# Retention's kept tiles on ScalarE's queue, and attention's gate by an exponential: a two-layer decoder in one launch

## The chip, the cores and the metric

The kernel runs on one core of one Trainium2 chip. The metric is the device time of one execution in microseconds (us), the median of three runs. Five engines work side by side, each in the order of its own instructions, and wait for each other by semaphores: TensorE (PE, with PEld for its weight loads), VectorE (DVE), ScalarE (ACT), GpSimd (POOL) and SyncE (SP). DMA transfers are issued by SP, POOL and, in the changed kernel, ACT, and run beside the engines.

## The reference

The trunk has two layers on 512 tokens of width 1024, all in 32-bit floats. Layer 0 mixes tokens by retention, layer 1 by forgetting attention. Each layer is: half a SwiGLU feed-forward, the mixer, half a SwiGLU feed-forward, a gated per-layer input. Cut to the two mixers:

```python
# retention, 4 heads, DK = 256, DV = 512
q, k, v, g = split(h @ w_in)
q, k = rotary(q), rotary(k) * DK ** -0.5
o = decayed causal (q k^T) v             # per head, decay gamma^(i - j)
y = silu(g) * rmsnorm(o, gn_w)           # norm over the head's 512 values
return y @ w_out

# forgetting attention, 16 heads of 64
q, k, v, fz = split(h @ w_in)
c = cumsum(log_sigmoid(fz + b_f))        # per head, over tokens
logits = q k^T * scale + c[i] - c[j]     # causal
return softmax(logits) @ v @ w_out
```

## The kernel before

Activations stand transposed, features on the 128 partitions and the 512 tokens along the row. Every product is made of three matmuls: each factor is split in a rounded half ("hi", a cast on ACT) and a rest ("lo", a subtraction on DVE), and hi·hi, hi·lo and lo·hi are summed in one of eight PSUM banks (`mm3`, L353 to L355). Feed-forward input products and most of retention's projections use one Strassen step (`product`, L557).

Weights are streamed by the class `Weights`: a plan lists all weight chunks in the order of use, SP loads a chunk raw, ACT casts its hi half (L88, or L134 and L135) and its lo half comes from DVE or POOL (L89), or from two ACT passes and an accumulating DMA on POOL (L136). There are three places for finished chunks; `take` gives the next chunk out and asks for those up to `look` (2) further on, so a chunk is cast when the chunk three before it has been used.

PE's order is that of the program text. The orders of the other engines are made by a planner at build time: among instructions that are ready in its own model of time it takes the one that stands earlier in the program. `tc.issue_after(x)` forces instructions of x's engine behind x. `with behind(last)` does so for a pair of instructions, one on ACT and one on DVE. On the chip each engine keeps the planned order, so an instruction whose input is late holds all that follow it on its engine.

Retention first makes q, k, v and gates of the heads 1 to 3 (and v of head 0) and keeps them in DRAM (`kept`, 28 pairs of tiles of 256 KB). Then, head by head: `scores` (four score blocks on PE, scaled and decayed by DVE at L911, split into `uhi` and `ulo` at L343 and L344), `attended` (48 matmuls of the split scores with v, the squares of the result on ACT at L937, their sum split), a part of the output projection of the head before (`out_blocks`), `head_scale` (mean of squares, root on ACT at L509, three Newton operations on DVE), more of the projection, `on_rows` (root to the rows: four PE transposes at L504 and an ACT copy at L957), and `outputs` (scale, gate, split). The next head's q, k and v come back from DRAM in `fetched`: a DMA on POOL (L853) puts a raw tile in what will be lo, ACT casts hi (L854), DVE subtracts (L855). `loaded(hd)` does it for a whole head; head 1's is called behind `attended` of head 0, later ones behind `attended` of the head before. The pool `ud` has 16 places: a head's q and k use 8 and its v 8 (4 of them elsewhere in heads 0 and 1).

Attention begins with the forget logits' product, `n.columns()` (root of the norm per token, in columns), the k product of the first pair of heads, `n.rows()` (columns to rows: PE transposes and an ACT copy), the q product. Then DVE and ACT work through log-sigmoid and cumulative sum on 16 rows, SP writes the sum to DRAM (`cdram`) and reads it back spread over all partitions (L1177). v is made in `v_block` (96 matmuls, split at L346 and L347), scores of pair 0 follow (L1169, L1172), softmax (DVE L1192 and L1196, ACT L1201 and L1203, POOL's causal mask L1178), then for each pair: k and q of the next pair, transposes of this pair's softmax (L1218), the product with v, scores of the next pair.

Of the kernel before, what the change touches and what calls it, by code (L numbers as in the profile page):

```python
# [18 lines left out]
S = 512  # L19
# [201 lines left out]
def trunk(ctx, tc, a):  # L221
# [18 lines left out]
    def unit(pool):  # L240
        return pool.tile([P, S], F32R, name="unit_" + {id(ua): "a", id(ub): "b", id(uc): "c", id(ud): "d"}[id(pool)])
# [265 lines left out]
    def rsqrt(out, v, t):  # L507

        root = nc.scalar.activation(t, v, AF.Sqrt)  # L509
        return root, newton(out, v, t)  # L510
# [8 lines left out]
    def mean_eps(out, total):  # L519
        nc.vector.tensor_scalar(out=out, in0=total, scalar1=1.0 / D, scalar2=EPS, op0=ALU.mult, op1=ALU.add)  # L520

    def proj(srcs, n, out=None, cols=slice(0, S), take=W.take):

        ws = [take(s) for s in srcs]
        os = out or [bank() for _ in ws]
        for k in range(KB):
            ks = slice(k * P, (k + 1) * P)
            for o, (wh, wl) in zip(os, ws):
                mm3(o, wh[:, ks], wl[:, ks], n.hi[k][:, cols], n.lo[k][:, cols], k == 0, k == KB - 1)
        return os  # L530
# [231 lines left out]
    def v_part(srcs, n):  # L762

        os = [bank() for _ in range(NT)]
        for c in range(4):
            wh, wl = W.take(srcs[c])
            for j in range(2):
                k = 2 * c + j
                js = slice(j * S, (j + 1) * S)
                for t in range(NT):  # L770
                    ts_ = slice(t * P, (t + 1) * P)
                    xh, xl = n.hi[k][:, ts_], n.lo[k][:, ts_]
                    nc.tensor.matmul(os[t], xh, wh[:, js], start=k == 0, stop=False)  # L773
                    nc.tensor.matmul(os[t], xh, wl[:, js], start=False, stop=False)  # L774
                    nc.tensor.matmul(os[t], xl, wh[:, js], start=False, stop=k == KB - 1)  # L775
        return os
# [16 lines left out]
    def retention(n, nxt, pools):  # L793
# [50 lines left out]
                nc.scalar.copy(t1, os[t])  # L844
                nc.gpsimd.dma_start(out=to[t // 2][:, t % 2, :], in_=t1)

        def fetched(src, low=ud, high=ud):

            out = []
            for s in range(2):  # L850
                hi, lo = unit(high), unit(low)
                raw = lo.bitcast(F32)
                nc.gpsimd.dma_start(out=raw, in_=src[:, s, :])  # L853
                nc.scalar.copy(hi, raw)  # L854
                nc.vector.tensor_tensor(out=lo, in0=raw, in1=hi.bitcast(F32), op=ALU.subtract)  # L855
                out.append((hi, lo))
            return out

        by7, got, dks = Strassen(n), {}, []

# [30 lines left out]
        sums.close()  # L891

        pool = stack.enter_context(tc.tile_pool(name="ret", bufs=1, reuse_waits="tile"))

        def loaded(hd):
            if hd == 0:
                return fetched(vd[0][0], ua) + fetched(vd[0][1], ua)
            q, kk = fetched(qd[hd]), fetched(kd[hd])
            return q, kk, fetched(vd[hd][0]) + (fetched(vd[hd][1], ub, ub) if hd == 1 else fetched(vd[hd][1]))

        def scores(hd, q, kk):
            dk, u = dks.pop(0), []
# [20 lines left out]
        @contextmanager  # L923
        def behind(last):
            with tc.issue_after(last[0].ins), tc.issue_after(last[1].ins):
                yield

        def attended(v, u):
            os = [bank() for _ in range(4)]
            for j in range(NT):  # L930
                for d, o in enumerate(os):
                    ds_ = slice(d * P, (d + 1) * P)
                    mm3(o[:, j * P : S], v[j][0][:, ds_], v[j][1][:, ds_], *u[j], j == 0, j == NT - 1)
            acc = None
            for d in range(4):
                sq = temp()
                nc.scalar.activation(sq, os[d], AF.Square)  # L937
                if acc is None:
                    acc = sq
                else:  # L940
                    nc.vector.tensor_tensor(out=acc, in0=acc, in1=sq, op=ALU.add)
            hi, lo = temp(F32R), temp(F32R)
            return os, (hi, lo), split(acc, hi, lo)

        def head_scale(parts):

            total = over_tokens(parts)
            v, t, rn = (pool.tile([P, NT], F32, name=x) for x in ("rv", "rt", "rn"))
            nc.vector.scalar_tensor_tensor(
                out=v, in0=total, scalar=1.0 / S, in1=epsc, op0=ALU.mult, op1=ALU.add  # L950
            )
            rsqrt(rn, v, t)
            return rn

        def on_rows(rn):
            rows = pool.tile([P, S], F32, name="rnrows")
# [44 lines left out]

        out_w, y = {}, [([], []) for _ in range(RH)]
        W.by_dma |= {id(x) for hd in (0, 1) for x in ret_o[hd]}
        v = loaded(0)
        u, _ = scores(0, got["q", 0], got["k", 0])
        sg = [gate(0)]
        os, acc, _ = attended(v, u)
        q, kk, v = loaded(1)
        sg.append(gate(1))
        rn = head_scale(acc)  # L1010
        (g,) = proj_forms(ret_g[0][2], n)
        rn, copied = on_rows(rn)
        with tc.issue_after(copied.ins):
# [3 lines left out]
        for hd in (1, 2, 3):  # L1017
            u, last = scores(hd, q, kk)
            with behind(last):
                outputs(hd - 1, os, sg, rn, y[hd - 1], range(1 if hd == 3 else 3, 4))  # L1020
            os, acc, last = attended(v, u)
            if hd < 3:
                with behind(last):
                    q, kk, v = loaded(hd + 1)
                sg = kept_gates(hd)
                out_blocks(hd - 1, y[hd - 1], range(0, 2))
                rn = head_scale(acc)
                out_blocks(hd - 1, y[hd - 1], range(2, 4))
                rn, _ = on_rows(rn)
                outputs(hd, os, sg, rn, y[hd], range(3 if hd == 1 else 1))  # L1030
                out_blocks(hd - 1, y[hd - 1], range(4, 8 if hd == 1 else 6))
# [1 line left out]
        out_blocks(1, y[1], range(6, 8))  # L1033
        both = OutBoth([(ret_o[2], *y[2]), (ret_o[3], *y[3])], nxt)
        both.first((0,))
        rn = head_scale(acc)
        both.first((1,))
        rn, _ = on_rows(rn)
        both.first((2, 3))
# [9 lines left out]
    def forgetting(n, nxt):  # L1049
        H = 64  # L1050
        with tc.tile_pool(name="fox", bufs=1, reuse_waits="tile") as pool:
# [3 lines left out]

            (fz,) = proj([a["fox_f"]], n)
            n.columns()
            begun = proj(fox_qk[0][0:1], n)
            n.rows()
            begun += proj(fox_qk[0][1:2], n)  # L1060

            z, e, u_, l, t_ = (temp()[0:FH] for _ in range(5))
# [5 lines left out]
            nc.scalar.activation(l, u_, AF.Ln)  # L1068
            nc.vector.tensor_scalar(out=t_, in0=u_, scalar1=-1.0, scalar2=None, op0=ALU.add)
            nc.vector.tensor_tensor(out=e, in0=e, in1=t_, op=ALU.subtract)  # L1070
            nc.vector.reciprocal(t_, u_)
            nc.vector.tensor_tensor(out=e, in0=e, in1=t_, op=ALU.mult)
            nc.vector.tensor_tensor(out=l, in0=l, in1=e, op=ALU.add)
            nc.vector.tensor_scalar(out=z, in0=z, scalar1=bf, scalar2=0.0, op0=ALU.add, op1=ALU.min)
            cur, new = temp()[0:FH], temp()[0:FH]
# [26 lines left out]
            def v_block(half):  # L1102

                vs = v_part(fox_v[half], n)
                W.low = nc.gpsimd
                out = []
                for t0 in range(0, NT, 2):
                    both = [[unit(ub).rearrange("p (h a d) -> p h a d", h=4, a=2) for _ in range(2)] for _ in range(2)]
                    for i in range(2):
                        for t, vt in zip((t0, t0 + 1), both):  # L1110
                            last = split(vs[t][:, i * H2 : (i + 1) * H2].rearrange("p (h d) -> p h d", h=4),
                                         vt[i][:, :, 0, :], vt[i][:, :, 1, :], n.c[:, t : t + 1])
                    out += both
                return out, last

            own = [slice(0, H), slice(H, P)]
# [472 lines left out]
```

## Time and profile before

| | us |
|---|---|
| median of 3 runs | 2135.58 (2134.19 to 2135.72) |
| the profiled execution | 2137.78 |
| its span, first to last instruction | 2135.9 |
| PE busy | 2111.0 (99% of the span) |
| DVE busy | 1576.9 (74%) |
| ACT busy | 1277.2 (60%) |
| POOL busy | 279.3 (13%) |
| mean granted clock of PE | 0.995 |

A row of a timeline has the start from the span's first instruction, the duration, the engine, the line of the code, the operation, out<-in by the program's names, the shapes, the count, and in square brackets the idle time of the engine before it and what ended that. A row of waits has the engine and its line, who was waited for, the total in us, how often, and the longest. A row of windows has the stretch, its length, the busy time of each engine with the count of its instructions, the granted clock of PE, the busy share of the 16 DMA engines and what they moved. PEq, ACTq or SPq stand for an engine's sequencer, which issues DMAs. Durations of matmuls overlap: one starts every 0.23 us or so at 512 columns while each is shown with 0.39.

### The profile page before, as it was taken

The numbers are of one execution on the slowest core, as the hardware profiler recorded it, in microseconds if no ns is written. First come the engines' busy times: TensorE is split into PE (matmuls) and PEld (weight loads), VectorE is DVE, ScalarE is ACT, GpSimd is POOL, SyncE is SP. The second block draws the span as 40 slices with busy tenths as digits, with TensorE's granted clock in tenths as the row PEclk, the third lists the DMA queues.
The fourth block names the chain that finished last, engine by engine and source line by source line (L and its number), as shares of the span: only waits on it lengthen the run. The fifth ranks groups of instructions, "written<-read, shape, count | busy, mean of one in ns | idle before, by whom it ended". The sixth has DMA issues, their size and how long they took to land.

```text
span 2135.9 us, 36254 instructions
## 1 busy us (share of the span) xinstructions
PE 2111.0 (99%) x14155; PEld 1938.3 (91%) x14155; DVE 1576.9 (74%) x2916; ACT 1277.2 (60%) x2201; POOL 279.3 (13%) x306
## 2 busy tenths in 40 slices
PE   9999999999998999999999999999999999999998
PEld 9999998999997898989989999998788899999988
DVE  9786868677666787868768686776675687867775
ACT  8474657545564563736557565555786774655555
POOL 0010100111311010201001010110243300101100
PEclk9999999999999999999999999999999999999999
DMA  6474654676765254746436565563422335755631
GB/s 196 124 176 137 159 139 135 174 197 189 221 188 156 81 131 125 183 133 166 130 93 154 133 169 149 143 149 109 119 68 91 104 98 131 177 140 145 157 109 40
DMA packets 104892, 299.97 MB, mean 140 GB/s; under 512 B 11136, under 2 KB 14720, under 8 KB 104720
## 3 DMA queue, kind: packets, MB, share of 16 engines
q1 hardware_dynamic: 65088, 212.92, 30.3%
q0 software_dynamic: 38400, 83.64, 20.7%
q8 instruction: 111, 1.82, 0.3%
q10 hardware_dynamic: 1232, 1.09, 0.2%
q14 instruction: 61, 0.50, 0.1%
HBM read 285.00 MB, written 12.62 MB: 139 GB/s over the span
## 4 chain that ended last, share of the span: by engine, by line
PE 88%; DVE 4%; issue 3%; DMA 2%; ACT 2%; POOL 1%; SPq 0%; POOLq 0%; ACTq 0%; DVEq 0%
PE bank L557 41%; PE bank L353 11%; PE bank L354 11%; PE bank L355 11%; PE bank L634 4%; PE bank L840 1%; PE bank L839 1%; PE bank L841 1%; DVE w L89 1%; DMA unit_d<-kept 1%; PE bank L1218 1%; PE bank L773 1%; PE bank L774 1%; PE bank L775 1%; PE bank L542 1%
## 5 line engine op out<-in xcount | busy, mean ns | idle before, releaser
L88 ACT CAST w<-wraw 128x1024 fp32r<-128x1024 f32 (+1 forms) x207 | 209.6, 1018 | 311.4 <-PE bank L355 206.8
L557 PE MATMUL bank<-unit_a,s 128*128 128x256 f32 x2202 | 322.7, 276 | 0.0
L89 DVE TENSOR_TENSOR s<-sums,s 128x512 fp32r<-128x512 f32 x372 | 246.4, 687 | 102.7 <-ACT s L88 102.0
L88 ACT CAST s<-sums 128x512 fp32r<-128x512 f32 x372 | 219.9, 618 | 167.9 <-PE bank L557 77.7
L557 PEld LDWEIGHTS bank<-unit_a,s 128*128 128x128 f32 x2202 | 284.9, 188 | 0.0
L353 PE MATMUL bank<-unit_d,w 128*128 128x512 f32 x656 | 255.7, 390 | 0.3 <-DVE tmp L1235 0.3
L354 PE MATMUL bank<-unit_d,w 128*128 128x512 f32 x656 | 255.3, 389 | 0.0
L355 PE MATMUL bank<-unit_d,w 128*128 128x512 f32 x656 | 255.2, 389 | 0.0
L89 DVE TENSOR_TENSOR w<-wraw,w 128x1024 fp32r<-128x1024 f32 (+1 forms) x186 | 218.4, 1175 | 46.8 <-ACT w L88 46.6
L557 PE MATMUL bank<-unit_b,s 128*128 128x256 f32 x1040 | 220.5, 276 | 0.0
L353 PE MATMUL bank<-unit_a,w 128*128 128x512 f32 (+1 forms) x536 | 199.8, 373 | 0.7 <-DVE unit_b L347 0.7
L355 PE MATMUL bank<-unit_a,w 128*128 128x512 f32 (+1 forms) x536 | 198.4, 370 | 0.9 <-DVE w L89 0.9
L354 PE MATMUL bank<-unit_a,w 128*128 128x512 f32 (+1 forms) x536 | 198.6, 370 | 0.1
L663 DVE SCALAR_TENSOR_TENSOR tmp<-bank,rows 128x512 f32<-128x512 f32 x96 | 66.2, 690 | 145.9 <-PE bank L355 145.8
L557 PEld LDWEIGHTS bank<-unit_b,s 128*128 128x128 f32 x1040 | 165.4, 188 | 0.0
L136 POOL DMA_DIRECT2D a<-in_ffn_w_in x80 | 70.9, 886 | 651.4 <-ACT a L135 471.6
L557 PE MATMUL bank<-unit_b,w 128*128 128x256 f32 x837 | 153.6, 282 | 0.0
L557 PE MATMUL bank<-unit_a,w 128*128 128x256 f32 x978 | 149.7, 278 | 0.0
L557 PE MATMUL bank<-unit_c,s 128*128 128x256 f32 x682 | 149.2, 276 | 0.0
L355 PEld LDWEIGHTS bank<-unit_d,w 128*128 128x128 f32 x656 | 123.1, 188 | 25.8
L353 PEld LDWEIGHTS bank<-unit_d,w 128*128 128x128 f32 x656 | 123.1, 188 | 25.6 <-DVE tmp L1235 0.5
L354 PEld LDWEIGHTS bank<-unit_d,w 128*128 128x128 f32 x656 | 123.1, 188 | 25.2
(352 smaller groups left out, 4846.6 us busy)
## 6 DMA issues: line engine op xcount, KB each, us to landing
wraw<-in_ffn_w_in SPq DMA_DIRECT2D x174, 512.0 KB, 4.4
wraw<-in_ffn_w_out SPq DMA_DIRECT2D x64, 512.0 KB, 4.3
w<-in_ffn_w_in POOLq DMA_DIRECT2D x57, 512.0 KB, 5.5
a<-in_ffn_w_in POOLq DMA_DIRECT2D x79, 256.0 KB, 6.2
wraw<-in_ret_p SPq DMA_DIRECT2D x28, 512.0 KB, 3.7
wraw<-in_ffn_w_out SPq DMA_DIRECT2D x32, 384.0 KB, 3.5
kept<-tmp POOLq DMA_DIRECT2D x40, 256.0 KB, 3.8
wraw<-in_ret_v SPq DMA_DIRECT2D x16, 512.0 KB, 4.5
```

Of the source, the lines that this page charges most:

```text
L88: self.cast = self.nc.scalar.copy(hi, raw)
L89: low.tensor_tensor(out=lo, in0=raw, in1=hi.bitcast(F32), op=ALU.subtract)
L136: self.nc.gpsimd.dma_start(out=lo, in_=src, accum_op=ALU.add)
L353: nc.tensor.matmul(out, wh, xh, start=first, stop=False)
L354: nc.tensor.matmul(out, wh, xl, start=False, stop=False)
L355: nc.tensor.matmul(out, wl, xh, start=False, stop=last)
L542: nc.tensor.matmul(o[:, half], w[:, ks], x, start=k == t == q == 0, stop=k == KB - 1 and q == 2, skip_group_check=True,)
L557: add = lambda w, x, start, stop: nc.tensor.matmul(out, w, x, start=start, stop=stop, skip_group_check=True)
L634: nc.tensor.matmul(o[:, HALVES[t]], x[:, ks], y, start=k == t == q == 0, stop=k == KB - 1 and q == 2, skip_group_check=True,)
L663: nc.vector.scalar_tensor_tensor(out=t1, in0=o, scalar=-0.5, in1=n.r, op0=ALU.mult, op1=ALU.mult)
L773: nc.tensor.matmul(os[t], xh, wh[:, js], start=k == 0, stop=False)
L774: nc.tensor.matmul(os[t], xh, wl[:, js], start=False, stop=False)
```

## The change

Retention: `fetched` is divided in `fetch`, which takes the places and issues the DMAs on ACT's queue (head 0's v stays on POOL's), and `halves`, which rounds. q and k of the next head are asked for behind the last split of this head's scores, and rounded behind `attended`. v is asked for behind `attended`, and rounded behind the root of `head_scale`, which now returns the instructions of the root. For head 1 the half of v that goes to the pool `ub` is asked for together with q and k.

Attention: `n.rows()` runs in the middle of the first k product, before its fifth of eight blocks. 1/u is computed as exp(-ln u), by ACT, where u = 1 + exp(-|z|) and ln u is there already, instead of DVE's reciprocal. In the v products one chunk less is asked for ahead at the last take (`W.look`), and that chunk is asked for behind v's last split (`W.emit`), at both calls of `v_block`.

```diff
-    def proj(srcs, n, out=None, cols=slice(0, S), take=W.take):
+    def proj(srcs, n, out=None, cols=slice(0, S), take=W.take, between={}):
...
         for k in range(KB):
             ks = slice(k * P, (k + 1) * P)
+            if k in between:
+                between[k]()
             for o, (wh, wl) in zip(os, ws):
@@ v_part
         for c in range(4):
+            W.look = LOOKAHEAD - (c == 3)
             wh, wl = W.take(srcs[c])
+            W.look = LOOKAHEAD
@@ retention
-        def fetched(src, low=ud, high=ud):
-            out = []
+        def fetch(src, low=ud, high=ud, queue=nc.scalar):
+            out = [(unit(high), unit(low)) for _ in range(2)]
             for s in range(2):
-                hi, lo = unit(high), unit(low)
+                queue.dma_start(out=out[s][1].bitcast(F32), in_=src[:, s, :])
+            return out
+
+        def halves(tiles):
+            for hi, lo in tiles:
                 raw = lo.bitcast(F32)
-                nc.gpsimd.dma_start(out=raw, in_=src[:, s, :])
                 nc.scalar.copy(hi, raw)
                 nc.vector.tensor_tensor(out=lo, in0=raw, in1=hi.bitcast(F32), op=ALU.subtract)
-                out.append((hi, lo))
-            return out
+            return tiles
...
-            rsqrt(rn, v, t)
-            return rn
+            return rn, rsqrt(rn, v, t)
...
-        v = loaded(0)
-        u, _ = scores(0, got["q", 0], got["k", 0])
+        v = halves(fetch(vd[0][0], ua, queue=nc.gpsimd) + fetch(vd[0][1], ua, queue=nc.gpsimd))
+        u, last = scores(0, got["q", 0], got["k", 0])
+        with behind(last):
+            q, kk, late = fetch(qd[1]), fetch(kd[1]), fetch(vd[1][1], ub, ub)
         sg = [gate(0)]
-        os, acc, _ = attended(v, u)
-        q, kk, v = loaded(1)
+        os, acc, last = attended(v, u)
+        with behind(last):
+            v = fetch(vd[1][0]) + late
+            halves(q + kk)
         sg.append(gate(1))
-        rn = head_scale(acc)
+        rn, last = head_scale(acc)
+        with behind(last):
+            halves(v)
...
         for hd in (1, 2, 3):
             u, last = scores(hd, q, kk)
             with behind(last):
+                if hd < 3:
+                    q, kk = fetch(qd[hd + 1]), fetch(kd[hd + 1])
                 outputs(hd - 1, os, sg, rn, y[hd - 1], range(1 if hd == 3 else 3, 4))
             os, acc, last = attended(v, u)
             if hd < 3:
                 with behind(last):
-                    q, kk, v = loaded(hd + 1)
+                    v = fetch(vd[hd + 1][0]) + fetch(vd[hd + 1][1])
+                    halves(q + kk)
                 sg = kept_gates(hd)
                 out_blocks(hd - 1, y[hd - 1], range(0, 2))
-                rn = head_scale(acc)
+                rn, last = head_scale(acc)
+                with behind(last):
+                    halves(v)
                 out_blocks(hd - 1, y[hd - 1], range(2, 4))
@@ forgetting
-            begun = proj(fox_qk[0][0:1], n)
-            n.rows()
+            begun = proj(fox_qk[0][0:1], n, between={4: n.rows})
             begun += proj(fox_qk[0][1:2], n)
...
-            nc.vector.reciprocal(t_, u_)
-            nc.vector.tensor_tensor(out=e, in0=e, in1=t_, op=ALU.mult)
+            nc.scalar.activation(u_, l, AF.Exp, scale=-1.0)
+            nc.vector.tensor_tensor(out=e, in0=e, in1=u_, op=ALU.mult)
@@ v_block
                     out += both
+                with tc.issue_after(last[0].ins):
+                    W.emit(W.used + LOOKAHEAD)
                 return out, last
```

More of the change, by code (lines that the diff above doesn't have):

```diff
@@ L893, in retention @@
         pool = stack.enter_context(tc.tile_pool(name="ret", bufs=1, reuse_waits="tile"))
[L895 to L899, printed above, removed]
         def scores(hd, q, kk):
@@ L1035, in retention @@
         both.first((0,))
-        rn = head_scale(acc)
+        rn, _ = head_scale(acc)
         both.first((1,))
```

## The prediction

> **What bounds the kernel now.** I read the page first (busy shares), then the waits of TensorE (PE), then the granted clock in chosen windows, then the timelines of the engines around each wait.
>
> ```profile
> span 2135.9 us, 36254 instructions
> PE 2111.0 (99%) x14155; PEld 1938.3 (91%) x14155; DVE 1576.9 (74%) x2916; ACT 1277.2 (60%) x2201; POOL 279.3 (13%) x306
> ...
> PE bank L353 <- ACT uhi L343: 7.6, 3, 4.5
> PE bank L1169 <- DVE q L1153: 3.2, 1, 3.2
> ...
> PE bank L354 <- DVE ulo L344: 0.8, 3, 0.4
> ```
>
> PE is the bound, and the change takes no matmul away. So it can win only PE's idle time, 24.9 us in all, and what that idle time does to the clock. Three waiting lines belong to places that the change touches: 7.6 + 0.8 us where a retention head starts to multiply its scores with v, and 3.2 us where attention starts the scores of its second pair of heads. Each wait, and the five windows behind them:
>
> ```profile
> 581.91 0.58 PE L353 MATMUL bank<-uhi,unit_d 128*128 128x512 f32 x1 [1.81 <-ACT uhi L343]
> ...
> 653.88 0.80 PE L353 MATMUL bank<-uhi,unit_d 128*128 128x512 f32 x1 [4.47 <-ACT uhi L343]
> ...
> 686.37 0.49 PE L353 MATMUL bank<-uhi,unit_d 128*128 128x512 f32 x1 [1.32 <-ACT uhi L343]
> ...
> 1535.49 0.58 PE L1169 MATMUL bank<-klo,q 128*128 128x256 f32 x1 [3.23 <-DVE q L1153]
> ...
> 582.19:585.60 3.41, 3.18 (x8) 2.29 (x8) 2.23 (x6) 1.13 (x3) 2.12 (x4) 0.50 0.66 216
> 653.87:657.28 3.41, 3.40 (x7) 2.44 (x8) 3.35 (x8) 1.08 (x3) 2.78 (x5) 0.50 0.62 177
> 688.00:691.41 3.41, 3.41 (x9) 2.64 (x8) 3.05 (x8) 0.30 (x1) 0.00 (x0) 0.50 0.01 2
> 1534.51:1541.33 6.82, 5.84 (x19) 5.03 (x20) 6.70 (x27) 5.88 (x13) 3.17 (x2) 0.50 0.00 0
> 614.07:617.48 3.41, 3.19 (x14) 2.43 (x14) 3.01 (x7) 0.97 (x3) 2.27 (x4) 1.00 1.02 250
> ```
>
> In a window row the first bracket counts PE's matmuls and the column 0.50 or 1.00 is the granted clock. Behind each of the four waits the clock is halved for one stretch of 3.41 us (6.82 in attention). The last row is the head that hardly waited: 14 matmuls there, 8, 7 and 9 in the others. So a wait costs its length and then a slow stretch.
>
> **Retention: what removes the waits.** ScalarE (ACT) runs in order, and in the first two cases it stood at a rounding copy of a kept tile (L854) whose transfer had not landed, with the scores' uhi behind it:
>
> ```profile
> 580.20 0.62 ACT L854 CAST unit_b<-unit_b 128x512 fp32r<-128x512 f32 x1 [3.26 <-DMA unit_b<-kept]
> ...
> 581.26 0.60 ACT L343 CAST uhi<-tmp 128x512 fp32r<-128x512 f32 x1
> ...
> 651.75 0.62 ACT L854 CAST unit_d<-unit_d 128x512 fp32r<-128x512 f32 x1 [4.75 <-DMA unit_d<-kept]
> ...
> 684.32 0.69 DVE L855 TENSOR_TENSOR unit_d<-unit_d 128x512 fp32r<-128x512 f32 x1
> 684.92 1.66 DVE L911 SCALAR_TENSOR_TENSOR tmp<-bank,rk,acc 128x512 f32<-128x512 f32 x3
> ```
>
> The third wait is its VectorE (DVE) form: a rounding's subtract (L855) stands ahead of the scores' first eviction (L911). The new code issues q and k on ACT behind the last split of the scores before, and rounds them only after the head's product, about 9 us later (the four squares end it). It issues v behind that product's last split and rounds it behind the root. All eight roundings of a head are then ordered ahead of the next scores, so nothing of them stands in front of uhi. The idle time removed is 7.6 + 0.8 = 8.4 us, less what stays. The head at 614 shows the floor, 0.23 us for ulo:
>
> ```profile
> 614.80 0.50 PE L354 MATMUL bank<-ulo,unit_d 128*128 128x512 f32 x1 [0.23 <-DVE ulo L344]
> ```
>
> Three such floors leave 7.7 us. The slow stretches cost between 3.41 x (14 - 9) / 14 = 1.2 and half of 3.41 = 1.7 us each; I take 1.5, so 4.5 for three (3.7 to 5.1). Sum for retention 12.2 us; bounds 0, if the waits stay, and 8.4 + 5.1 = 13.5.
>
> [...]
>
> **Retention: what it adds.** 24 of the 28 reads of kept tiles leave POOL's queue for ACT's. POOL no longer has to reach them behind its weight transfers (L136). On ACT an issue holds the engine's order for about 0.4 us, by its only such rows, at the end of the kernel:
>
> ```profile
> 2114.37 0.40 ACTq L1444 DMA_DIRECT2D outT<-hall  x1
> ...
> DMA to landing us min/median/max: 2.9/7.0/10.9
> ...
> DMA to landing us min/median/max: 5.6/8.6/12.4
> ```
>
> The two landing rows are POOL's kept reads and SP's reads of the kept gates, the same 256 KB on the hardware queue. I take 8.6 us. The places asked for are free by construction: q and k go where the scores just finished had theirs, so no issue should stand at a place. 24 x 0.43 = 10 us more on ACT; it is covered by ACT's idle time (3.26 and 4.75 us of it stand in the two rows above), except around the root. There, in head 1:
>
> ```profile
> 624.91 0.62 ACT L343 CAST tmp<-tmp 128x512 fp32r<-128x512 f32 x1 [1.36 <-DVE tmp L941]
> 625.44 1.14 ACT L854 CAST unit_d<-unit_d 128x512 fp32r<-128x512 f32 x2
> 627.96 1.05 ACT L134 CAST w<-wraw 128x1024 fp32r<-128x1024 f32 x1 [1.38 <-PE bank L355]
> ...
> 630.49 1.28 ACT L509 ACT_TABLE_LOAD   x1
> 631.79 0.20 ACT L509 ACTIVATE rt<-rv 128x4 f32<-128x4 f32 x1
> ...
> 632.84 0.16 DVE L517 SCALAR_TENSOR_TENSOR rn<-rt,rn 128x4 f32<-128x4 f32 x1
> ...
> 634.15 0.60 PE L504 MATMUL bank<-ident,rn 128*128 128x128 f32 x4
> ...
> 640.06 0.39 PE L353 MATMUL bank<-unit_a,w 128*128 128x512 f32 x1
> ...
> DMA to landing us min/median/max: 6.6/7.0/9.5
> ```
>
> New order, in the old times: split to 625.5, four issues (1.7), four copies of q and k (4 x 0.52 = 2.1), the weight's two passes (2.0), table (1.3), root (0.2): 632.8 against 632.0. VectorE's last step to the root (L517) ended 1.0 us after ACT's, so now near 633.8 to 634.0, and PE asks for it at 634.15: it just fits. The weight cast at 627.96 goes on through POOL's accumulating transfer (last row: 7.0 us, at worst 9.5) and its low half is wanted by the third matmul after 640.06, at 640.5. Cast 1.4 us later, at 629.3, it is done at 631.3 and lands near 638.6: 1.9 us of cover, gone if the transfer takes its longest. For these two thin covers I book 0.8 us (0 to 1.6: nothing, or twice that).
>
> v is late next: its reads are issued from 625.5 to 627.2 and land by 8.6 us near 635.4, after the root. ACT then stands at v's first copy for up to 3 us, with the copy of the root's rows and later weight casts behind it. Rows and weights are wanted a chunk or more later, if the cast of 627.96 stays ahead of v, so I book nothing; rival B prices the other order.
>
> [...]
>
> **Attention.** The second pair's scores hang on the first pair's softmax, and that on this chain:
>
> ```profile
> 1499.12 3.34 DVE L1071 RECIPROCAL tmp<-tmp 16x512 f32<-16x512 f32 x1
> ...
> 1517.40 0.86 ACT L346 ACTIVATE unit_b<-bank,cols 128x256 fp32r<-128x256 f32 x2
> ...
> 1518.56 0.47 PE L353 MATMUL bank<-unit_a,w 128*128 128x512 f32 x1 [0.35 <-DVE unit_b L347]
> ...
> 1520.98 0.29 DVE L1192 CUSTOM_DVE_ANT_0 p<-bank,unit_c 128x128 f32<-128x128 f32 x1 [2.17 <-DMA unit_c<-cdram]
> ...
> 1521.58 2.41 POOL L89 TENSOR_TENSOR w<-wraw,w 128x1024 fp32r<-128x1024 f32 x1
> ...
> 1531.02 0.57 ACT L1134 CAST khi<-bank 64x512 fp32r<-64x512 f32 x1
> ```
>
> The softmax of pair 0 starts when the cumulative gate comes back from memory (1520.98); its exponentials hold ACT until the khi copy at 1531.02, and PE's scores of pair 1 wait to 1535.49. Moving the rows from behind a projection to its half takes 12 matmuls off, at the 14 in 3.41 us of above 2.9 us; the root of the columns must then be there earlier too, which costs PE some tenths at most, inside what I leave below. The reciprocal's 3.34 goes; an exponential of the same 512 elements (ACT's nearest row of that width: 0.62) and, bounded by the table row above, a load of 1.28 come. That is 2.9 + 3.3 - 1.9 = 4.3 us earlier, more than the 2.17 that VectorE waited; so v's own rounding (ACT's last ends at 1518.3, VectorE's half a microsecond later) sets the start, about 2.2 us sooner. POOL's weight subtract (2.41 at 1521.58), which now runs between its two masks, stands behind them. The second weight of pair 1 is cast after v's split (L88, 1.05 like 627.96) and subtracted by POOL (2.41): done near 1518.3 + 1.1 + 2.4 = 1521.8, or 1524.2 with another such subtract ahead of it; its projection starts 24 matmuls, 5.6 us, after 1518.56, at 1524.2. This cover is thin as well. I take 2.9 of the 3.23 and leave 0.3. The same edit at the second half of v meets the same work and I book nothing. The slow 6.82 us falls too: 16 matmuls of scores took 4.95 us there,
>
> ```profile
> 1515.51:1518.22 2.71, 2.71 (x17) 2.20 (x15) 1.78 (x5) 2.71 (x6) 0.00 (x0) 1.00 0.97 188
> 1535.49:1540.44 4.95, 4.95 (x16) 4.33 (x17) 4.89 (x17) 4.01 (x9) 2.28 (x1) 0.50 0.00 0
> ```
>
> against 2.71 warm: 2.2, and 0.4 in the 0.9 us of slow clock left. Attention: 2.9 + 2.6 = 5.5 us (bounds 0, and 3.2 + 3.4 = 6.6).
>
> **Sum.** 12.2 + 5.5 - 0.8 = 16.9 us. The profiled execution took 2137.78 us, span 2135.9; that is 2.2 above the median of the runs, 2135.58. 2137.8 - 16.9 = 2120.9, by the median **2118.7**.
>
> **Rivals.** (B) *The wait moves to v's landing in head 1.* If the planner puts v's copies ahead of the weight cast of 627.96, ACT stands until 635.4; copies (2.1), casts (2.0) and the transfer (0.3 and 7.0) end at 646.8 against 640.5: 6.3 us and 1.5 of slow clock, 7.8 back: 2126.5. For it: 8.6 us of landing against 6.3 between issue and root. Against: today that cast, ready first, comes first. (C) *Attention's wait shrinks but stays over 1 us*, with its slow stretch, because the added cast and the exponentials still end late: 5.5 becomes about 1.5, 2122.7. The wait of 1.32 us that sufficed for a slow stretch speaks for it. (D) *It doesn't do what it says:* roundings are still planned in front of uhi, only attention wins: 2130. For it: the order of today has the same fault, by a plan that takes transfers as landed too early. Against: the edges behind the root. (E) *Slower.* B's mechanism with transfers that land far later, since ACT's and SP's reads now crowd into one stretch: each further microsecond of landing is one of PE's at the weight wanted at 640.5. B stands at 8.6; the gain of 16.9 is used up at 8.6 + 16.9 - 7.8 = 17.7 us of landing, and the longest kept read took 12.4. At 25 us: 7.8 + 16.4 = 24.2 back, 2143.
>
> **Numbers.** Forecast 0.60 (its own range 2115 to 2122), B 0.15, C 0.10, D 0.07, E 0.08. Low end: all bounds taken, 13.5 + 6.6 = 20.1, so 2115.5, less a microsecond for runs: 2114.5. High end 2128 takes in C and B and leaves D and E out. Over 0.2% (4.3 us) is about what a measurement of this kernel tells from no change: forecast, B, C and half of D are faster, 0.88; half of D the same, 0.04; E slower, 0.08.
>
> **What would show it.** Right: PE's three waits on uhi gone to 0.3 us or less, clock 1.00 through 570 to 700 and 1500 to 1550; kept reads on ACT's queue, landing 7 to 9 us later; VectorE's first L1192 without a wait on cdram; one table load after Ln and none before the softmax. Wrong: a new PE wait on a weight in head 1's out blocks (B), on q L1153 (C), uhi behind a rounding copy (D).

## The result, and the profile after

The changed kernel takes 2118.41 us (median of four runs, 2117.90 to 2118.82), the kernel before on the same chip 2134.89 us (four runs, 2133.82 to 2135.72). The ratio is 0.9923, with a 95% interval of 0.9906 to 0.9940: 16.5 us less. The forecast was 2118.7.

The page's first lines and TensorE's waits in the kernel after:

```profile
span 2117.0 us, 36225 instructions
...
PE 2102.4 (99%) x14155; PEld 1932.4 (91%) x14155; DVE 1573.0 (74%) x2915; ACT 1276.7 (60%) x2201; POOL 266.6 (13%) x282
```

```profile
PE bank L1180 <- DVE q L1164: 0.9, 2, 0.6
PE bank L504 <- DVE rn L517: 0.9, 1, 0.9
...
PE bank L354 <- DVE ulo L344: 0.6, 2, 0.4
```

The three waits on uhi, 7.6 us in all, are gone; of the wait on q 0.9 us are left in two parts, and the wait on rn is new. TensorE's idle time is 2117.0 - 2102.4 = 14.6 us where it was 24.9, and its busy time is 8.6 us less with the same 14155 matmuls: that second part is the clock, since the four slow windows of before make 3 x 3.41 + 6.82 = 17.05 us at 0.50, half of which is 8.5, and none of them is left. The four windows that answer to the slow ones of before (first bracket TensorE, then the granted clock in the column behind POOL's):

```profile
579.61:583.02 3.41, 3.41 (x18) 2.92 (x17) 1.92 (x2) 1.58 (x2) 0.00 (x0) 1.00 0.95 317
645.98:649.39 3.41, 3.41 (x18) 2.93 (x18) 3.19 (x8) 0.74 (x3) 0.00 (x0) 1.00 0.76 187
675.35:678.76 3.41, 3.04 (x13) 2.31 (x13) 3.04 (x8) 0.97 (x3) 0.00 (x0) 1.00 0.38 135
...
1518.69:1522.10 3.41, 2.50 (x15) 2.04 (x15) 3.32 (x6) 3.36 (x8) 0.00 (x0) 1.00 0.00 0
```

All stand at 1.00, with 13 to 18 matmuls. Before, the three of retention had 7 to 9, and attention's had 19 in twice the time. Now the same matmuls of TensorE in both timelines, first of before, then of after: the first of a head's products (L353), the transposes that end retention's heads (L504), and the first score of attention's third pair.

```profile
614.07 0.50 PE L353 MATMUL bank<-uhi,unit_d 128*128 128x512 f32 x1
...
708.21 0.60 PE L504 MATMUL bank<-ident,rn 128*128 128x128 f32 x4
...
1556.40 0.60 PE L1169 MATMUL bank<-klo,q 128*128 128x256 f32 x2
```

```profile
579.61 0.40 PE L353 MATMUL bank<-uhi,unit_d 128*128 128x512 f32 x1
...
609.68 0.50 PE L353 MATMUL bank<-uhi,unit_d 128*128 128x512 f32 x1
...
630.84 0.32 PE L504 MATMUL bank<-ident,rn 128*128 128x128 f32 x1 [0.86 <-DVE rn L517]
...
645.98 0.45 PE L353 MATMUL bank<-uhi,unit_d 128*128 128x512 f32 x1
...
675.35 0.49 PE L353 MATMUL bank<-uhi,unit_d 128*128 128x512 f32 x1
...
695.59 0.60 PE L504 MATMUL bank<-ident,rn 128*128 128x128 f32 x4
...
1538.02 0.37 PE L1180 MATMUL bank<-klo,q 128*128 128x256 f32 x1
```

Subtracting, with the rows of 581.91, 634.15, 653.88 and 686.37 shown ahead of the prediction: the changed kernel is ahead by 2.30 us at head 0's product, 4.39 at head 1's, 3.31 at head 1's transposes (1.1 lost there, 0.86 of it in a wait that is new), 7.90 at head 2's product, 11.02 at head 3's, 12.62 behind retention and 18.38 behind attention's second pair. So retention gave 12.6 us and attention 5.8. These are the shifts of one pair of profiles. The profiled runs end 2137.78 - 2118.82 = 18.96 apart; the medians, 16.5.

### The profile page after: what moved, and what is told of

Read it like the earlier page. It is cut to its first block, busy times and chain, and to the rows that moved or that the text cites. A ratio compares the mean times of both kernels' runs of the same rounds, so it can differ in the third digit from the quotient of the medians.

```text
span 2117.0 us, 36225 instructions
## 1 busy us (share of the span) xinstructions
PE 2102.4 (99%) x14155; PEld 1932.4 (91%) x14155; DVE 1573.0 (74%) x2915; ACT 1276.7 (60%) x2201; POOL 266.6 (13%) x282
## 3 DMA queue, kind: packets, MB, share of 16 engines
HBM read 284.47 MB, written 12.62 MB: 140 GB/s over the span
## 4 chain that ended last, share of the span: by engine, by line
PE 88%; DVE 4%; issue 4%; ACT 2%; DMA 1%; POOL 0%; SPq 0%; POOLq 0%; ACTq 0%; DVEq 0%
PE bank L559 41%; PE bank L354 12%; PE bank L353 12%; PE bank L355 12%; PE bank L636 4%; PE bank L544 1%; DMA w<-in_ret_p 1%; PE bank L843 1%; PE bank L844 1%; PE bank L845 1%; PE bank L777 1%; PE bank L778 1%; PE bank L779 1%; PE bank L1229 1%; DVE w L89 1%
## 5 line engine op out<-in xcount | busy, mean ns | idle before, releaser
L353 PE MATMUL bank<-unit_d,w 128*128 128x512 f32 x656 | 255.7, 390 | 0.3 <-DVE tmp L1246 0.3
L353 PE MATMUL bank<-unit_a,w 128*128 128x512 f32 (+1 forms) x536 | 199.4, 372 | 0.0
L353 PEld LDWEIGHTS bank<-unit_d,w 128*128 128x128 f32 x656 | 123.2, 188 | 25.8 <-DVE tmp L1246 0.5
```

The source lines that it names most:

```text
L353: nc.tensor.matmul(out, wh, xh, start=first, stop=False)
```

## The experiments

Each run is compared with the kernel before on its own chip. Medians, ratios and 95% intervals:

| run | us | before there | ratio | interval |
|---|---|---|---|---|
| the change | 2118.41 | 2134.89 | 0.9923 | 0.9906 to 0.9940 |
| e1 retention's part alone | 2124.88 | 2133.15 | 0.9954 | 0.9939 to 0.9968 |
| e2 attention's part alone | 2127.67 | 2133.15 | 0.9971 | 0.9957 to 0.9986 |
| e3 reads on POOL's queue | 2118.02 | 2133.15 | 0.9921 | 0.9906 to 0.9936 |
| e4 v rounded ahead of the root | 2123.41 | 2133.15 | 0.9951 | 0.9936 to 0.9965 |
| e5 reciprocal | 2119.71 | 2135.53 | 0.9922 | 0.9905 to 0.9938 |
| e6 rows behind the projection | 2119.85 | 2135.53 | 0.9920 | 0.9901 to 0.9940 |
| e7 weight's place as before | 2120.82 | 2135.53 | 0.9928 | 0.9911 to 0.9944 |
| e10 root ahead of the hall sums | 2117.17 | 2135.53 | 0.9910 | 0.9894 to 0.9926 |
| e11 only the weight's place | 2119.96 | 2134.20 | 0.9936 | 0.9918 to 0.9954 |
| e12 v read behind the root | 2130.17 | 2134.20 | 0.9982 | 0.9973 to 0.9992 |

The two with added copies, e8 and e9, ran once each: 2132.85 and 2133.61 us.

**The two halves by themselves.** e1 takes the three edits of attention back, e2 takes retention back to the old `fetched` and `loaded`.

```diff
 # e1, against the changed kernel
-            W.look = LOOKAHEAD - (c == 3)
...
-            begun = proj(fox_qk[0][0:1], n, between={4: n.rows})
+            begun = proj(fox_qk[0][0:1], n)
+            n.rows()
...
-            nc.scalar.activation(u_, l, AF.Exp, scale=-1.0)
+            nc.vector.reciprocal(t_, u_)
...
-                with tc.issue_after(last[0].ins):
-                    W.emit(W.used + LOOKAHEAD)
```

> Retention's edits alone; attention as before. My sum says 12.2 - 0.8 = 11.4 us of the gain are retention's: 2134.9 - 11.4 = 2123.5 us, with the granted clock at 1.00 from 570 to 700 us and the 3.2 us wait on q L1153 and its slow stretch still there. Rival: the two parts help each other (attention's waits fall only because retention shifted the phase of the slow stretches): then it is below 2121 or above 2126.

> Attention's edits alone; retention as before. My sum: 5.5 us, 2134.9 - 5.5 = 2129.4 us, the waits on uhi (1.8, 4.5 and 1.3 us) and their slow stretches unchanged. If the parts add, this gain and that of retention alone make the whole 16.5 within 1 us.

TensorE's waits in e1, then in e2:

```profile
1524.59 0.61 PE L1177 MATMUL bank<-klo,q 128*128 128x256 f32 x2 [2.95 <-DVE q L1161]
...
1527.06 0.98 PE L1177 MATMUL bank<-klo,q 128*128 128x256 f32 x2 [0.90 <-DVE q L1161]
```

```profile
653.70 0.80 PE L353 MATMUL bank<-uhi,unit_d 128*128 128x512 f32 x1 [6.08 <-ACT uhi L343]
...
686.58 0.50 PE L353 MATMUL bank<-uhi,unit_d 128*128 128x512 f32 x1 [1.63 <-ACT uhi L343]
```

Each half keeps the waits of the other, and removes its own. On that chip retention alone is worth 0.46% and attention alone 0.29%; together 0.75%, against 0.79% for e3, which has both. So the parts add, as far as intervals of about 0.15% to either side (3 us) can tell. By the medians attention gave the 5.5 us that were expected, but retention 8.3 (9.8 by the ratio) where 11.4 were: the 12.6 us above are more than this chip's runs show, and the sum of the two medians, 13.8, is 1.4 short of e3's 15.1, where the expectation had allowed 1. e2 also shows that the old waits are not the same in every execution: the same retention code waited 1.81, 4.47 and 1.32 us in the profile of before, and hardly at all, 6.08 and 1.63 here.

**The queue, or the places in the text.**

```diff
-        def fetch(src, low=ud, high=ud, queue=nc.scalar):
+        def fetch(src, low=ud, high=ud, queue=nc.gpsimd):
```

> The changed kernel with the kept tiles asked for on POOL's queue again, the places in the text of asking and of rounding as changed. Theory (the order of rounding is what counts, landing depends little on the queue): within 1 us of 2118.4. Rival (ScalarE's queue is what counts, because POOL reaches its issues late, behind its weight transfers): the roundings stand at late tiles again and PE waits at uhi or at weights, at least one wait over 1.3 us with a slow stretch, 2121 to 2130.

```diff
 # e4, for head 1; the loop over the heads has the same move
             v = fetch(vd[1][0]) + late
-            halves(q + kk)
+            halves(q + kk + v)
...
         rn, last = head_scale(acc)
-        with behind(last):
-            halves(v)
```

> The changed kernel, but v is rounded together with q and k behind the head's product instead of behind the root. Theory (ScalarE would stand at v's landing ahead of the root and the weight casts): the root comes 2 to 4 us later, PE's wait at the transposes of the root (0.9 us in the changed kernel) grows to 2 or more with a slow stretch in one or two heads: 2121 to 2125. Rival (v lands in about 4 us on this queue, in time): 2118.4 within 0.6.

e3 left the gain whole: 2118.02 us on POOL's queue, 2118.41 on ScalarE's. It did so with reads that took longer to land, 7.1 us in the middle against 4.7. The spread of landing times of line L855 in the kernel after, and in e3 (each with the four reads that both leave on POOL):

```profile
DMA to landing us min/median/max: 2.6/4.7/8.8
```

```profile
DMA to landing us min/median/max: 3.8/7.1/13.3
```

These landing times compare more than two queues. `behind` ties the instructions of ScalarE and VectorE alone, so on POOL's queue the planner asked earlier and in larger bunches: for head 2's q and k from 603.53 us on (611.46 in the kernel after), for its v from 609.75 (620.60). What the two kernels share is the order of the roundings, and that the reads are there in time. e4 shows from the other side that the order counts: with v's four copies ahead of the root, TensorE waits for the root in heads 0, 1 and 2, 1.55, 1.46 and 2.67 us, where four copies of 0.54 take 2.2, and the time is 5.4 us above e3's. ScalarE stood at late tiles of v for 0.42 us at most, so it is the copies and not the landing, against that run's theory. No run has the early reads with the roundings in their old places, so how much of the gain on q and k comes from each is not shown.

```profile
PE bank L504 <- DVE rn L517: 5.7, 3, 2.7
```

**The new wait in head 1.** The change brought one wait of 0.86 us, for the root's last step (L517). VectorE's and ScalarE's timelines of the kernel after, around it:

```profile
628.63 0.16 DVE L516 SCALAR_TENSOR_TENSOR rt<-rt,rv 128x4 f32<-128x4 f32 x1
630.03 0.69 DVE L999 TENSOR_TENSOR hall<-bank,hall 128x512 f32<-128x512 f32 x1 [1.23 <-PE bank L355]
630.63 0.15 DVE L517 SCALAR_TENSOR_TENSOR rn<-rt,rn 128x4 f32<-128x4 f32 x1
```

```profile
620.60 1.93 ACTq L855 DMA_DIRECT2D unit_d<-kept  x4
622.58 2.18 ACT L861 CAST unit_d<-unit_d 128x512 fp32r<-128x512 f32 x4 [1.36 <-DMA wraw<-in_ret_o]
...
627.98 0.20 ACT L509 ACTIVATE rt<-rv 128x4 f32<-128x4 f32 x1
628.10 2.16 ACT L861 CAST unit_d<-unit_d 128x512 fp32r<-128x512 f32 x4
```

ScalarE's root is done at 628.2 and VectorE's third step at 628.8; then VectorE stands for 1.23 us at a sum into hall, whose bank TensorE has not finished, with the root's fourth step queued behind it. e10 orders those sums behind the root:

```diff
-                out_blocks(hd - 1, y[hd - 1], range(2, 4))
+                with tc.issue_after(last[1].ins):
+                    out_blocks(hd - 1, y[hd - 1], range(2, 4))
```

> The changed kernel with one order more: the sums of the out blocks 2 and 3 are ordered behind the last Newton step of the head's root. Theory (in head 1 an addition into hall, at 630.03 with a wait of 1.23 us on a bank of PE, stands between two steps of the root on VectorE; PE's wait of 0.86 us on rn L517 comes from that alone): the wait goes, 0.6 to 0.9 us less, 2117.5 to 2117.8. Rival (the root is late because of ScalarE, or the hall sums are then late for PE's banks): no gain, 2118.4 or up to 1 us more, with the wait moved to a bank that the sums free.

The wait is gone, and in the trace nothing takes its place in VectorE's order:

```profile
629.64 0.16 DVE L516 SCALAR_TENSOR_TENSOR rt<-rt,rv 128x4 f32<-128x4 f32 x1
629.84 0.16 DVE L517 SCALAR_TENSOR_TENSOR rn<-rt,rn 128x4 f32<-128x4 f32 x1
```

The ratio is 0.9910 against 0.9923; the intervals overlap, so a gain of a microsecond is what the trace says and the times only allow.

**How late may v be?** The prediction took v's reads to land behind the root and booked that at nothing. In the kernel after they don't: ScalarE issues v at 620.60 and goes from the root straight into its copies (628.10). e12 makes v later than that, and later than the prediction had it, by asking for v behind the root:

```diff
 # for head 1's v; the loop over the heads has the same move
         with behind(last):
-            v = fetch(vd[1][0]) + late
             halves(q + kk)
...
         rn, last = head_scale(acc)
         with behind(last):
+            v = fetch(vd[1][0]) + late
             halves(v)
```

> The changed kernel with the reads of v asked for behind the root of a head instead of behind its product, so that they land behind the root in every head, and ScalarE stands at v's first copy; in head 1 the second pass of the weight wanted for out block 2 is then ordered behind two or three of v's copies. Theory (rows and weights behind v are wanted a chunk or more later; rival B of the prediction applies only where the weight's transfer is behind v): reads land 3 to 5 us after their issue, ScalarE stands 2 to 4 us per head, the weight's transfer in head 1 starts 4 to 6 us later than 630 and lands near 642 to 644; PE wants it 4 us before: a wait of 2 to 5 us and one or two slow stretches of 1.5 each: 2121 to 2126. Rival (there is cover enough everywhere, as the term booked at nothing has it): within 1 us of 2118.4, no new wait over 1 us.

ScalarE's timeline of e12, and TensorE's:

```profile
620.30 4.74 ACTq L855 DMA_DIRECT2D unit_d<-kept  x2
625.09 0.62 ACT L343 CAST unit_a<-tmp 128x512 fp32r<-128x512 f32 x1 [8.96 <-DMA unit_d<-kept]
...
639.27 0.62 ACT L861 CAST unit_d<-unit_d 128x512 fp32r<-128x512 f32 x1 [4.11 <-DMA unit_d<-kept]
642.67 0.62 ACT L861 CAST unit_d<-unit_d 128x512 fp32r<-128x512 f32 x1 [2.78 <-DMA unit_d<-kept]
644.60 0.62 ACT L861 CAST unit_d<-unit_d 128x512 fp32r<-128x512 f32 x1 [1.31 <-DMA unit_d<-kept]
...
655.22 1.04 ACT L343 CAST uhi<-tmp 128x512 fp32r<-128x512 f32 x2 [1.73 <-DVE tmp L911]
```

```profile
625.76 0.49 PE L353 MATMUL bank<-unit_a,w 128*128 128x512 f32 x1 [1.26 <-ACT unit_a L343]
...
655.89 0.50 PE L353 MATMUL bank<-uhi,unit_d 128*128 128x512 f32 x1 [3.36 <-ACT uhi L343]
```

ScalarE stands 4.11 + 2.78 + 1.31 = 8.2 us at v's copies in head 1, and the ratio rises to 0.9982: three quarters of the gain are gone. The theory had the sign but not the place. TensorE doesn't wait for the weight of out block 2. The delay goes on through VectorE's order as well as ScalarE's: v's subtracts (L862) wait for the copies, behind them VectorE works without a pause from 645.25 until it evicts the next scores (L911, at 654.45), ScalarE waits 1.73 us for that, and uhi comes 3.36 us late. So the old wait is back by another way; in the next head it is 1.62 us.

The first two rows are a second effect, which isn't v's lateness. ScalarE computed nothing for 8.96 us, because the third and fourth of four issues for the next head's q and k began only at 620.30 and 624.72. Each began 0.02 us after a read of a kept gate (L973, on SP's queue) had landed, at 620.28 and 624.70, and the trace gives each issue and that read the same semaphore (104 and 107). SP had asked for these two reads at 610.91 and 611.86. In the kernel after the same pairs share a semaphore, but SP asks at 603.25 and 604.20, and both have landed (611.50 and 612.71) when ScalarE gets there (612.47 and 613.01). The two issues brought TensorE the wait of 1.26 us above; so e12's price is not v's lateness alone.

**Attention, edit by edit.**

> The changed kernel with VectorE's reciprocal put back in the place of the added exponential. Theory (the softmax of pair 0 now starts when v's split has ended, at 1505.5, and the cumulative gate is already there: its copies were issued at 1493.9 to 1496.4): 3.3 us of reciprocal against 1.9 us of exponential and table load, so the gate comes 1.4 us later. It was read at 1496.4 and is wanted at 1505.5; with 5 to 8 us of landing it still comes in time or misses by at most a microsecond: 2118.4 to 2120. Rival (the exponential is the part that carries attention's gain): VectorE waits for the gate again by over 1 us, PE waits over 1 us on q L1164 and the slow clock comes back: 2122 to 2124.

> The changed kernel with the rows of the norm put back behind the whole first projection (12 matmuls, 2.9 us, later). Theory (v's split sets the start of the softmax, the gate has some microseconds of cover left): the gate lands 2.9 us later and takes most of that cover; PE's wait on q grows from 0.9 to between 1 and 2.5 us, 2119 to 2122. Rival (the gate has more cover than that): no difference, within 0.7 of 2118.4. Other rival (the move is what carries the gain): the whole 5.5 us come back, 2124.

> The changed kernel with the second weight of pair 1 cast where it was before (the two edits of the weight's place undone), rows and exponential as changed. Theory (that edit keeps the weight's two passes, 2.0 on ScalarE and 2.4 on POOL, from standing between the softmax's own steps): PE waits 1 to 3 us for a half of q or for the weight, with one or two slow stretches of 3.41 us (1.5 each): 2120 to 2124. Rival (the weight is cast in time wherever it stands): within 0.7 of 2118.4.

> The changed kernel with two of attention's three edits undone (rows of the norm behind the first projection, reciprocal for the exponential); only the second weight's place is as changed. Each of the two alone, put back, cost about a microsecond: with the reciprocal the gate landed at 1504.9 and 1505.7, when v's split ended; with the late rows at 1507.5 and 1508.1 beside a split ending at 1508.5. Theory (the two take their time from the same cover, so the second one is what counts): the gate lands 2 to 4 us behind v's split, PE waits 2 to 4 us on q, with one or two slow stretches, 2121 to 2124. Rival (each edit has its own price of about a microsecond, and the weight's place carries the rest): 2120 to 2121, PE's waits on q under 1.6 us, no slow stretch.

VectorE's first step of the softmax, in the kernel after and in e1:

```profile
1505.47 0.28 DVE L1203 CUSTOM_DVE_ANT_0 p<-bank,unit_c 128x128 f32<-128x128 f32 x1
```

```profile
1510.39 0.29 DVE L1200 CUSTOM_DVE_ANT_0 p<-bank,unit_c 128x128 f32<-128x128 f32 x1 [2.28 <-DMA unit_c<-cdram]
```

The edits of e5, e6 and e7 are the three of e1, each by itself; e11 takes back the rows and the exponential. None of the four differs from the whole by more than its interval, while taking all three back does: e1 and e3, on one chip, have intervals that don't meet. What each edit does is in the traces. In e6 the gate came 1507.5 and 1508.1, v's split ended at 1508.5, and TensorE waited 0.61 us for q, as it does with the rows early: by itself that move shows no effect. e5 went as neither theory had it. The gate was there in time, VectorE began at 1505.87 without a wait, and yet q came 2.01 us late and a slow stretch came with it. The reason is on ScalarE; the table loads of e5 and then of the kernel after:

```profile
1505.33 1.99 ACT L88 CAST w<-wraw 128x1024 fp32r<-128x1024 f32 x2
1507.34 1.28 ACT L1212 ACT_TABLE_LOAD   x1
1508.63 0.51 ACT L1212 ACTIVATE p<-p,sm 128x256 f32<-128x256 f32 x1
```

```profile
1475.20 1.28 ACT L1074 ACT_TABLE_LOAD   x1
...
1478.09 1.28 ACT L1077 ACT_TABLE_LOAD   x1
...
1480.50 1.28 ACT L1080 ACT_TABLE_LOAD   x1
```

In both kernels the tables change once more between the logarithm and the softmax. With the reciprocal that load (1.28 us) stands ahead of the softmax's first exponential, on the path; the added exponential of 16 rows draws it to 1480.50, where nobody waits. The number of loads is the same, three. In the kernel before the load stood ahead of the softmax too (L1201, at 1518.28), but hidden: the first exponential waited for VectorE until 1522.06. e11 shows the same load as e5 (1508.16) and the same wait of 2.01, with a slow stretch; its gate was there in time, so neither of its two expectations held. In e7 a cast of the weight stands inside v's split, TensorE waits 0.35 us twice for v's halves, and 0.77 and 0.91 us for q. So the edits cover for one another: of TensorE's waits the exponential takes away 1.4 us and a slow stretch, the weight's place 1.5 us, the rows by themselves nothing. The gate comes late as well only where all three are missing, in the kernel before and in e1: there VectorE stood 2.17 and 2.28 us for it. Part of that is landing: e1's two reads of the gate took 6.3 and 6.5 us, those of e5 and e11 3.1 to 3.5; the runs don't show why. The pairs that leave out the weight's place and one more edit were not run.

**What stood ahead of the slow stretches.** e4 raised the question: a wait of 2.67 us and no slow stretch, when 1.32 us had sufficed in the profile of before. In before the slow stretches begin at 582.19, 653.87, 688.00 and 1534.51 us. That is 71.68, 34.13 and 846.51 us apart, 21, 10 and 248 times 3.413. Two runs with useless copies on ScalarE, ahead of the first uhi of heads 1, 2 and 3, vary the wait:

```diff
+                if j == 0:
+                    for _ in range({1: 2, 2: 4, 3: 6}.get(hd, 0)):   # e9: 1: 5, 2: 7, 3: 3
+                        nc.scalar.copy(t1[:, :w], t1[:, :w])
                 last = split(t1[:, :w], hi, lo)
```

> The changed kernel with copies that change nothing put on ScalarE ahead of the first uhi of a head's scores: 2, 4 and 6 of 0.5 to 0.6 us in heads 1, 2 and 3; TensorE then waits there about 1.1, 1.5 and 3.3 us, and the clock is watched. Theory (the chip looks at stretches of 3.413 us on a fixed grid; one in which TensorE was idle 1.7 us or more is followed by a stretch at half clock; in ten traces 1.70 to 3.41 was, 1.60 and less wasn't): heads 1 and 2 none (unless another wait falls into the same stretch), head 3 slow if one stretch of the grid holds 1.7 us of its wait, which it does for nearly all phases. Rival (the length of one wait decides, from somewhere over 1.3 us): heads 2 and 3 slow whatever the grid. Second rival (a whole stretch of 3.4 us must be idle): none slow. Time 2118.4 plus the waits of about 6 us plus 1.5 per slow stretch: 2124 to 2128.

> As the run with 2, 4 and 6 copies, with 5, 7 and 3 in heads 1, 2 and 3: waits of about 2.8, 3.1 and 1.6 us. Theory (half of a stretch of 3.413 us on a fixed grid): head 3 not slow; heads 1 and 2 slow where one stretch of the grid holds over 1.7 us of the wait and not slow where a boundary of the grid cuts it into parts below that; which one follows from the starts of the segments of the clock in the same trace. Rival (length of a wait): heads 1 and 2 slow, and head 3 perhaps. Second rival (a whole idle stretch): none. Time 2118.4 plus 7.5 plus 1.5 per slow stretch: 2125 to 2130.

The waits came out longer than meant (e8: 1.67, 2.23 + 0.57 and 4.45 us; e9: 3.69, 4.18 and 2.50 + 0.57), and the times with them, above both forecasts (three and four slow windows beside 8.9 and 10.9 us of waits). Windows laid on such a grid of 3.413 us in each trace: of before the one ahead of its third slow stretch, then two of e4, then of e8:

```profile
684.59:688.00 3.41, 1.72 (x9) 1.18 (x8) 3.41 (x7) 1.86 (x4) 0.00 (x0) 1.00 0.46 154
```

```profile
666.05:669.46 3.41, 1.86 (x9) 1.21 (x7) 2.96 (x8) 2.37 (x4) 0.85 (x1) 1.00 0.26 52
669.47:672.88 3.41, 2.30 (x12) 2.00 (x13) 1.98 (x5) 0.59 (x1) 0.00 (x0) 1.00 1.01 233
```

```profile
611.75:615.16 3.41, 2.24 (x9) 1.62 (x10) 3.07 (x7) 1.26 (x5) 0.00 (x0) 1.00 1.09 288
649.30:652.71 3.41, 0.76 (x2) 0.45 (x3) 3.11 (x7) 2.03 (x5) 0.00 (x0) 1.00 0.77 187
652.71:656.12 3.41, 3.41 (x9) 2.64 (x9) 0.97 (x2) 0.62 (x1) 0.00 (x0) 0.50 1.02 302
...
686.85:690.26 3.41, 2.40 (x5) 1.60 (x6) 3.41 (x6) 1.79 (x4) 0.00 (x0) 0.50 0.01 2
690.26:693.67 3.41, 3.41 (x10) 2.64 (x9) 1.50 (x3) 0.62 (x1) 0.00 (x0) 0.50 0.00 0
```

In the window of before a smaller gap (0.37 us, for ulo) lies beside the wait of 1.32 us, only 1.72 us of work are left, and the slow stretch of 688.00 follows. e4's 2.67 us were cut by a boundary into 1.6 and 1.1: TensorE is busy 1.86 us in the first window as shown (1.81 on the grid proper, 0.05 us later), and the clock stays. In e8 the window from 649.30 has 0.76 us of work, and the next is slow; the one from 611.75 has 2.24, and nothing follows. Neither rival holds: e8's first head waited 1.67 us without a slow window, more than the 1.32 that had one in before, and no window had to be wholly idle (2.65 us of 3.41 sufficed in e8's second head). e9's third head was expected to stay at full clock and didn't; its wait was 2.5 us, not 1.6, and the window from 687.05 has 0.88 us of work, so 2.53 idle, more than the theory's 1.7.

## Why the prediction was right, and where its reasons were not

- *The clock behind a wait is part of its price.* Right, and a little larger. From the table of starts: behind its wait head 0 gained 4.39 - 2.30 = 2.1 us (0.23 of it a wait for ulo), head 2 11.02 - 7.90 = 3.1 less head 3's own wait of 1.3, so 1.8, and head 3 12.62 - 11.02 = 1.6, where 1.5 each was taken.
- *Retention, 12.2 us less 0.8.* Measured 12.6 in the pair of profiles, the lost microsecond of head 1 included, and 8.3 to 9.8 by e1's runs. The waits on uhi went to nothing; two floors of ulo stay, of 0.23 and 0.37 us, not three of 0.23.
- *The thin cover at head 1's root.* It failed, where the working said that it just fits. The 0.8 us were booked for two covers together; that one wait of 0.86 us matches them is luck, since the engine is another. The sum had ScalarE's root move from 632.0 to 632.8 by old times, and ScalarE was in time; a sum into hall stood between two steps of the root on VectorE, and e10 takes the wait away by that order alone. The other cover, the weight's, held.
- *v lands by 8.6 us, behind the root; ScalarE stands there for up to 3 us at no cost.* The step that failed. In place all reads landed in 2.6 to 8.8 us, 4.7 in the middle, and v's own in 2.6 to 5.1, by the time the root was done. Whether up to 3 us would have been free is not shown. More is not: in e12 the reads of v for the heads 2 and 3 take 5.0 to 9.8 us, ScalarE stands 8.2 us in head 1, and with the held issues 11.8 us of the gain go (2130.17 against 2118.41). Rival B, which did not arise in place, had the direction, but the waiter is uhi and not a weight. The times of e3 and of the kernel after agree, 2118.02 and 2118.41; whether a read lands sooner by the one queue than by the other they can't tell, since e3 asked for its reads at other times.
- *Attention, 5.5 us.* Measured 5.8, for a reason that the sum had only in part. v's split does set the start, and the gate is there before. But the working credited the exponential with bringing the gate 1.4 us earlier, which no one needed (e5, e6), and left out that, once the gate is in time, it takes a table load of 1.28 us off the softmax's path. The prediction did name the sign of it, no load ahead of the softmax, without pricing it.
- *The rest of the shift.* The medians gained 16.5 where the profiles lie 18.96 apart. The profiled run of before was one of its slower ones, by 2.2 to 2.9 us. So it is in part luck that 2118.7 came within 0.3 us: the profiles moved by 2.1 us more than the sum's 16.9, and the slow profiled run took about as much back. e2 fits this: how long the old waits are, and how many slow stretches follow, changes from run to run.
- *Rivals.* D fell (no rounding in front of uhi), C fell (0.59 and 0.32 us, without a slow stretch), B and E did not arise; e12 shows that their direction, later reads, is real.

## What to carry to other kernels

Where a transfer's consumer and critical work stood in the order of one engine, the gain came from ordering the consumer behind the critical work and asking early enough, more than from the queue that carried the transfer. The queue made 0.4 us (e3, 2118.02 against 2118.41), v's copies ahead of the root cost 5.4 (e4 against e3), and v's reads behind the root, with two held issues, 11.8 (e12). In e12 two issues on ScalarE began only when reads of SP's queue had landed, and ScalarE computed nothing for 8.96 us; so look at what the issues themselves wait for. Before pricing an activation by its own duration, find where the next table load falls: the added exponential was worth its place because the load of 1.28 us that stands at 1507.34 without it (e5) stands at 1480.50 with it. And price a wait of TensorE with the slow clock behind it: in the three heads of before 1.6 to 2.1 us came on top of waits of 1.32 to 4.47, and in e4 none on top of 2.67.

## What the runs showed of the hardware that was not expected

TensorE's waits were not followed by a slow clock according to their length. On the grid of 3.413 us above, these windows stood at 1.00 and were followed by one at 0.50, with TensorE idle in them for:

| trace | window from (idle, us) |
|---|---|
| before | 578.77 (1.81), 650.45 (3.41), 684.59 (1.69), 1531.10 (2.32) |
| e5 | 1519.69 (1.72) |
| e8 | 649.30 (2.65), 683.43 (3.41) |
| e9 | 608.54 (2.17) |
| e12 | 425.00 (1.86), 653.71 (2.41) |

Followed by 1.00 was e4's window from 666.05, idle for 1.55 us as shown and 1.60 on the grid proper, and in the kernel after, which has no slow window between 30 and 2100 us, the most is 1.18 (from 2047.42). A window at 0.50 was followed by another where TensorE was idle in it for 0.98 us (before, from 1534.51), 1.01 (e8, 686.85) and 1.51 (e9, 611.96), and by one at 1.00 where it was idle for 0.23 (before, 582.19). So a wait of 1.32 us had a slow stretch behind it where another gap lay in its window, and one of 2.67 us had none where a boundary cut it. These are the windows of this kernel's traces; what in the chip sets the clock they don't show.
